# One transformer block on one core: the first layer norm in pairs of blocks, the modulation's scale in four column groups, and a set of weight loads issued from ACT

## The chip, the cores and the metric

The kernel runs on one core of one Trainium2 chip. The metric is device time in microseconds: the median of three runs. A core has engines with instruction queues of their own, which run side by side and wait for each other by semaphores: TensorE (PE, with its weight loads shown as PEld), VectorE (DVE), ScalarE (ACT), GpSimd (POOL) and SyncE (SP). SP does no arithmetic here, it issues DMA transfers; ACT and POOL can issue them too.

## The reference

The reference is one block of depth one over 512 tokens of width 1024: a layer norm modulated by a condition vector, an attention and gating mixer, a second modulated layer norm and a mixture of experts. The change touches the condition's modulation and the first layer norm.

```python
mod = jax.nn.silu(c) @ w_ada[l] + b_ada[l]
sh1, sc1, gt1, sh2, sc2, gt2 = [m[:, None, :] for m in jnp.split(mod, 6, axis=-1)]
h = _layernorm(x) * (1.0 + sc1) + sh1
mix = _token_mixers(h, ...)
x = _layernorm(DN_ALPHA * x + gt1 * mix, ln1_g[l], ln1_b[l])
h = _layernorm(x) * (1.0 + sc2) + sh2
ffn = _peer(h, ...)
x = _layernorm(DN_ALPHA * x + gt2 * ffn, ln2_g[l], ln2_b[l])
```

So mod is a row of six parts of 1024: sh1 and sc1 are wanted at once, before the first projection h @ w_in; the other four later.

## The kernel before

The 512 tokens are four blocks (b = 0 to 3) of 128 rows, x_102 to x_108 in the lists of order below. The width of 1024 is eight chunks of 128 (k = 0 to 7). A projection needs h with the width on the partitions, so x is normalized (L278), transposed by PE in 32 pieces into PSUM (xtr, L283) and copied by ACT to xnT (L284). The modulation is then applied to xnT, one chunk at a time: h_hi (L304) scales and shifts on ACT and casts to the high part hT_h, h_lo (L308) subtracts on DVE for the low part hT_l. Every projection is three products, w_h with hT_h, w_l with hT_h, w_h with hT_l (mm3c, L226), where w_h and w_l are the two parts of a weight that ACT casts (L88) and DVE subtracts (L89). The first projection is w_k: its first half (k = 0 to 3) runs inside the block that the change rewrites, with four accumulators gk, its second half and w_v after it.

The modulation's first two parts, shift (part 0) and scale (part 1), are made in two halves (hf) of 512 columns each, which serve k = 0 to 3 and k = 4 to 7. Each half and part has eight chunks of weights, in two tiles of 1 MB: ada_w for the first half, ada_b for the second, all of them issued by SP (L293). There are two ways to make a row. On DVE (ada_c, L117), eight steps each multiply a chunk by a column of scT (the condition) and add to ada_acc, which ada_t (L108) then sums over the partitions, by PE products with a column of ones (ada_pt) that also turn the row into columns. On PE, eight products with scT as the stationary operand sum straight into one row (ada_row, L313), which ACT copies out. Before, the scale of the first half goes over PE and the three others over DVE; those of the second half stand between the h_lo steps of the first four chunks, and their column sums before the products of k = 3 (L328). ada_e (L299) makes both parts' columns and adds one to the scale (sc1p, L302).

The four later parts are made by ada (L123) in the attention's time: DVE sums into ada_acc, PE sums its partitions in two products of 512 columns with one row out (L135), ACT copies the two rows (L137).

In this first block the order on PE, DVE and ACT is the order of the code; SP's and POOL's orders, and that of all engines outside of such blocks, are set by a scheduler. A DMA transfer tells of its landing by one of eight semaphores (DMAHW0 to DMAHW7), taken in turn in the scheduler's order; the issue of a transfer waits until the earlier transfer with the same semaphore has landed.

Of the kernel before, what the change touches and what calls it, by code (L numbers as in the profile page):

```python
# [9 lines left out]
F32 = mybir.dt.float32  # L10
# [7 lines left out]
ALU = mybir.AluOpType  # L18
# [36 lines left out]
def tile_block(ctx: ExitStack, tc: tile.TileContext, io: dict, out: bass.AP, dbg=None):  # L55
# [52 lines left out]
    def ada_t(acc, part, k0, n):  # L108

        pt = fbank("ada_pt")  # L110
        for c in range(n):
            mm(pt[:, c:c + 1], acc[:, c * P:(c + 1) * P], ones[0:acc.shape[0]], start=True, stop=True)
# [10 lines left out]
    def ada(pl, wl, part, tag, nw):  # L123
# [9 lines left out]
        pr = [fbank("ada_pr") for _ in range(2)]  # L133
        for hf in range(2):
            mm(pr[hf][0:1], ones, acc[:, hf * 512:(hf + 1) * 512], start=True, stop=True)  # L135
        for hf in range(2):
            cp(acc[0:1, hf * 512:(hf + 1) * 512], pr[hf][0:1])  # L137
# [127 lines left out]
    with ExitStack() as es:  # L265
# [8 lines left out]
        with tc.manual_schedule(engines={ET.PE, ET.DVE, ET.Activation}):  # L274
            ln = [(rs, neg(mu, rs)) for mu, rs in ln_stats(xs, D)]
            w_k = [load_w(wp, io["w_k"][0], 408)]
            for b, (rs, nm) in enumerate(ln):
                act(xs[b], xs[b], AF.Identity, scale=rs, bias=nm)  # L278
            for b in range(NB):
                for q in range(2):  # L280
# [3 lines left out]
                    cp(xnT[:, q * 4:q * 4 + 4, b * P:(b + 1) * P], pt.rearrange("p (c t) -> p c t", c=4))  # L284
            bt = [big("ada_b0", F32), big("ada_b1", F32)]
            sc1p = const.tile([P, KC], F32, name="sc1p")
            wa = [[[ap0.tile([P, 4, 512], F32, name="ada_w", bufs=4) for _ in range(2)] for _ in range(2)],
                  [[bt[part][:, c4 * 4:c4 * 4 + 4] for c4 in range(2)] for part in range(2)]]
            acc = [[ap0.tile([P, 512], F32, name="ada_acc", bufs=3) for _ in range(1 + hf)] for hf in range(2)]
            for hf in range(2):  # L290
                for part in range(2):
                    for c4 in range(2):
                        dma(wa[hf][part][c4], io["w_ada01"][hf, part, c4])  # L293

            def ada_cs(hf, part, c0, c1):
                for c in range(c0, c1):
                    ada_c(acc[hf][part], wa[hf][part][c // 4][:, c % 4], c)
# [13 lines left out]
            pr = fbank("ada_row")  # L311
            for c in range(KC):
                mm(pr[0:1], scT[:, c:c + 1], wa[0][1][c // 4][:, c % 4], start=c == 0, stop=c == KC - 1)  # L313
            row = ap0.tile([1, 512], F32, name="ada_row", bufs=1)
            cp(row, pr[0:1])
            acc[0].append(row)
            ada_cs(0, 0, 0, KC)
            ada_cs(1, 0, 0, 4)
            ada_e(0)
            gk = [bank("g") for b in range(NB)]  # L320
# [972 lines left out]
```

## Time and profile before

| | |
|---|---|
| median of 3 runs | 1711.72 us (1710.55 to 1711.78) |
| profiled execution | 1708.1 us |
| its span, first to last instruction | 1706.4 us |
| PE busy | 1660.3 us, 97% |
| DVE busy | 1365.5 us, 80% |
| ACT busy | 663.3 us, 39% |
| PE's idle time before its first transpose | 14.77 us |

An engine's busy time counts its own work and not the issuing of transfers or waiting. The 3% in which PE is not busy are for the most part the start: the first slices of the page show PE at 6 tenths, and every later one at 9 until the last. All times in the rows are from the span's start, for one profiled execution; the runs' median is 3.6 us above it.

### The profile page before, as it was taken

The page shows a single profiled execution, that of the slowest core. Times are in us where ns is not written, and L with a number is a line of the kernel's source. Part 1 is how long each engine was busy: PE and PEld are TensorE (multiplying, and loading weights), DVE is VectorE, ACT ScalarE, POOL GpSimd, SP SyncE. Part 2 cuts the span into 40 slices and gives each one's busy share as a digit, 9 for nine tenths or more (in the row PEclk, how much of TensorE's full clock was granted, in tenths as well). Part 3 has the DMA queues.
Part 4 walks back from the last instruction along what each step waited for, and adds up shares of the span by engine and source line. Part 5 has one row for each costly group of instructions (what it writes and reads, how often), then busy time and mean ns, then how long its engine had stood idle before and what let it go on. Part 6 is the DMA issues. An engine that isn't in the chain of part 4 may idle for free.

```text
span 1706.4 us, 24481 instructions
## 1 busy us (share of the span) xinstructions
PE 1660.3 (97%) x9145; PEld 1434.6 (84%) x9145; DVE 1365.5 (80%) x2682; ACT 663.3 (39%) x1029; POOL 356.7 (21%) x276
## 2 busy tenths in 40 slices
PE   6999999999999999999999999999999999999997
PEld 4977766677888899999998999999999998887785
DVE  6534777758879999998875888888798889788898
ACT  4523532343342244455453333333333334333332
POOL 0000000000000000000011554555454544324310
PEclk9999999999999999999999999999999999999999
DMA  7411344433342145587788999999999999999993
GB/s 307 172 56 50 124 179 155 154 118 136 142 162 79 35 149 168 176 293 263 260 297 321 337 346 359 362 350 355 355 349 345 348 324 347 369 380 384 375 340 121
DMA packets 164478, 424.31 MB, mean 249 GB/s; under 512 B 17283, under 2 KB 84099, under 8 KB 156551
## 3 DMA queue, kind: packets, MB, share of 16 engines
q1 hardware_dynamic: 119159, 277.29, 46.2%
q0 software_dynamic: 36992, 134.25, 21.1%
q10 hardware_dynamic: 8208, 11.21, 1.8%
q8 instruction: 71, 1.16, 0.3%
q14 instruction: 48, 0.39, 0.1%
HBM read 381.59 MB, written 41.11 MB: 248 GB/s over the span
## 4 chain that ended last, share of the span: by engine, by line
PE 88%; DVE 5%; DMA 4%; ACT 1%; issue 1%; SPq 1%; DVEq 0%; ACTq 0%
PE y L1106 24%; PE a_ps L755 10%; PE a_ps L754 10%; PE a_ps L757 10%; PE gf L228 3%; PE gf L229 3%; PE gf L230 3%; PE g_ps L1012 3%; PE s L515 2%; PE qh L782 2%; PE qh L783 2%; PE qh L785 2%; PE oacc L558 2%; DMA gA<-gA_d 1%; DMA v_f<-in_peer_vT_dram 1%; PE g L230 1%
## 5 line engine op out<-in xcount | busy, mean ns | idle before, releaser
L1106 PE MATMUL y<-v_hl,w_eh 128*128 128x512 f32 x1536 | 375.8, 391 | 2.9 <-ACT w_eh L1095 2.6
L754 PE MATMUL a_ps<-h2T_h,u_hl 128*128 128x384 f32 x1024 | 344.2, 336 | 3.1 <-ACT u_hl L88 3.1
L755 PE MATMUL a_ps<-h2T_l,u_hl 128*128 128x384 f32 x1024 | 344.8, 337 | 0.4 <-DVE h2T_l L89 0.3
L1106 PEld LDWEIGHTS y<-v_hl,w_eh 128*128 128x128 f32 x1536 | 287.0, 188 | 63.0 <-ACT w_eh L1095 5.0
L1038 POOL DMA_INDIRECT grow<-in_peer_u_dram,eidx x128 | 172.2, 1345 | 462.1 <-ACT u_hl L88 276.2
L1090 ACT CAST v_hl<-v_f 128x1024 fp32r<-128x1024 f32 x128 | 134.7, 1052 | 266.8 <-PE y L1106 156.6
L1038 POOL DMA_INDIRECT grow<-in_peer_v_dram,eidx x128 | 172.9, 1351 | 224.3 <-DVE yacc L1055 192.5
L757 PE MATMUL a_ps<-h2T_h,u_hl 128*128 128x384 f32 x1024 | 200.3, 335 | 0.0
L1106 PE MATMUL y<-v_hl,w_el 128*128 128x512 f32 x768 | 198.2, 389 | 0.0
L754 PEld LDWEIGHTS a_ps<-h2T_h,u_hl 128*128 128x128 f32 x1024 | 192.3, 188 | 5.7 <-ACT u_hl L88 3.4
L755 PEld LDWEIGHTS a_ps<-h2T_l,u_hl 128*128 128x128 f32 x1024 | 192.3, 188 | 3.3 <-DVE h2T_l L89 1.0
L89 DVE TENSOR_TENSOR u_hl<-u_f,u_hl 128x1024 fp32r<-128x1024 f32 x128 | 156.4, 1222 | 32.8 <-ACT u_hl L88 32.7
L1047 DVE SCALAR_TENSOR_TENSOR grow<-grow,h2t 128x1024 f32<-128x1024 f32 x128 | 153.2, 1223 | 34.0 <-DMA grow<-in_peer_u_dram,eidx 33.5
L757 PEld LDWEIGHTS a_ps<-h2T_h,u_hl 128*128 128x128 f32 x1024 | 179.0, 188 | 0.0
L1055 DVE SCALAR_TENSOR_TENSOR yacc<-grow,dact,yacc 128x1024 f32<-128x1024 f32 x128 | 164.0, 1281 | 18.5 <-DMA grow<-in_peer_v_dram,eidx 17.0
L1096 DVE TENSOR_TENSOR v_hl<-v_f,v_hl 128x1024 fp32r<-128x1024 f32 x128 | 156.2, 1220 | 20.7 <-ACT v_hl L1090 19.0
L1106 PEld LDWEIGHTS y<-v_hl,w_el 128*128 128x128 f32 x768 | 144.1, 188 | 30.2 <-DVE w_el L1097 0.3
L88 ACT CAST u_hl<-u_f 128x1024 fp32r<-128x1024 f32 x128 | 133.8, 1046 | 0.6 <-DMA u_f<-in_peer_uT_dram 0.6
L758 ACT ACTIVATE gA<-a_ps 128x384 f32<-128x384 f32 x119 | 58.4, 491 | 173.3 <-PE a_ps L757 167.7
L1095 ACT CAST w_eh<-gA 128x384 fp32r<-128x384 f32 x119 | 61.1, 514 | 150.5 <-DVE gA L1092 122.6
L1092 DVE TENSOR_TENSOR gA<-gA,g_rd 128x384 f32<-128x384 f32 x119 | 66.0, 554 | 35.0 <-DMA gA<-gA_d 34.1
L228 PE MATMUL gf<-w_h,hT_h 128*128 128x512 f32 x192 | 77.1, 403 | 0.0
(311 smaller groups left out, 2424.1 us busy)
## 6 DMA issues: line engine op xcount, KB each, us to landing
u_f<-in_peer_uT_dram SPq DMA_DIRECT2D x128, 512.0 KB
v_f<-in_peer_vT_dram SPq DMA_DIRECT2D x128, 512.0 KB
gdram<-g_st SPq DMA_DIRECT2D x12, 2048.0 KB
g_rd<-gdram SPq DMA_DIRECT2D x96, 256.0 KB
ada_w<-in_w_ada_dram SPq DMA_DIRECT2D x20, 1024.0 KB
gA_d<-gA ACTq DMA_DIRECT2D x57, 192.0 KB
gA<-gA_d SPq DMA_DIRECT2D x57, 192.0 KB
w_f<-in_w_merge_dram SPq DMA_DIRECT2D x8, 1024.0 KB
```

The lines of the kernel that those rows point to most:

```text
L88: i = cp(hi, src)
L89: V.tensor_tensor(lo, src, hi.bitcast(F32), op=ALU.subtract)
L228: mm(acc, lhs[0][:, k, tb], w[0][:, c, 0:n], start=k == 0, stop=False)
L754: mm(a, wh[:, k], h2T[0][:, k, T0:T0 + TD], start=k == 0, stop=False)
L755: mm(a, wh[:, k], h2T[1][:, k, T0:T0 + TD], start=False, stop=False)
L757: st["u"] = mm(a, wl[:, k], h2T[0][:, k, T0:T0 + TD], start=False, stop=k == KC - 1)
L1038: nc.gpsimd.indirect_dma_start(out=t[:, :], out_offset=None, in_=io["peer_u" if n < P else "peer_v"], in_offset=bass.IndirectOffsetOnAxis( ...
L1047: V.scalar_tensor_tensor(t, t, 1.0, h2t, op0=ALU.mult, op1=ALU.mult, accum_out=G["da"][:, k:k + 1])
L1055: V.scalar_tensor_tensor(yacc, G[P + k], G["da"][:, k:k + 1], yacc, op0=ALU.mult, op1=ALU.add)
L1090: cp(vh, v)
L1096: V.tensor_tensor(vl, v, vh.bitcast(F32), op=ALU.subtract)
L1106: mm(yps[i][hf], w[:, i * P:(i + 1) * P], v[:, hf * 512:(hf + 1) * 512], start=e == 0 and n == 0, stop=e == P - 1 and n == 2)
```

## The change

The first layer norm's statistics are no longer made for all four blocks before the first is normalized. Two blocks at a time are normalized, and their transposes and copies follow; the third and fourth blocks' square roots and normalizations come after copies of the first two on ACT. Each block has its own square root and scale steps (128x1) instead of one set for four (128x4).

The scale (part 1) goes over PE in both halves (ada_row(hf)), the shift (part 0) over DVE in both. The eight products of a row are written to four PSUM rows, 0, 32, 64 and 96, two products each, so that each of four groups of 32 array columns makes one; a memset clears the bank ahead, ACT copies the whole bank, and the sum over partitions in ada_t adds the four rows. In ada the same is done with pieces of 256 columns.

The second half's four weight tiles (ada_b) are issued by ACT, after the normalization of the second block, and no longer by SP. The w_k weights' low part is made in four steps beside h_lo; the second half's DVE steps come after these, its row product before k = 3, its column sums after k = 3.

```diff
-            mm(pt[:, c:c + 1], acc[:, c * P:(c + 1) * P], ones[0:acc.shape[0]], start=True, stop=True)
+            mm(pt[:, c:c + 1], acc[:, c * P:(c + 1) * P], ones, start=True, stop=True)
...
-        pr = [fbank("ada_pr") for _ in range(2)]
-        for hf in range(2):
-            mm(pr[hf][0:1], ones, acc[:, hf * 512:(hf + 1) * 512], start=True, stop=True)
-        for hf in range(2):
-            cp(acc[0:1, hf * 512:(hf + 1) * 512], pr[hf][0:1])
+        pr = fbank("ada_pr")
+        for j in range(4):
+            mm(pr[j * 32:j * 32 + 1, 0:256], ones, acc[:, j * 256:(j + 1) * 256], start=True, stop=True)
+        for j in range(4):
+            cp(acc[0:1, j * 256:(j + 1) * 256], pr[j * 32:j * 32 + 1, 0:256])
...
-            ln = [(rs, neg(mu, rs)) for mu, rs in ln_stats(xs, D)]
-            w_k = [load_w(wp, io["w_k"][0], 408)]
-            for b, (rs, nm) in enumerate(ln):
-                act(xs[b], xs[b], AF.Identity, scale=rs, bias=nm)
-            for b in range(NB):
+            pr = [bank("ada_row") for _ in range(2)]
+            for t in pr:
+                V.memset(t, 0.0)
+            def x_tr(b):
                 for q in range(2):
                     pt = bank("xtr")
...
+            for b0 in range(0, NB, 2):
+                bs = range(b0, b0 + 2)
+                mv = [ln_mv([xs[b]], D) for b in bs]
+                rs = [rsqrt_eps(m[:, :, 1], 1) for m in mv]
+                nm = [neg(m[:, 0, 0:1], r) for m, r in zip(mv, rs)]
+                if b0:
+                    x_tr(b0 - 1)
+                for i, b in enumerate(bs):
+                    act(xs[b], xs[b], AF.Identity, scale=rs[i], bias=nm[i])
+                if b0 == 0:
+                    for part in range(2):
+                        for c4 in range(2):
+                            nc.scalar.dma_start(bt[part][:, c4 * 4:c4 * 4 + 4], io["w_ada01"][1, part, c4])
+                x_tr(b0)
+            x_tr(NB - 1)
+            w_k0 = load_f(wp, io["w_k"][0], 408)
...
-            for hf in range(2):
-                for part in range(2):
-                    for c4 in range(2):
-                        dma(wa[hf][part][c4], io["w_ada01"][hf, part, c4])
+            for part in range(2):
+                for c4 in range(2):
+                    dma(wa[0][part][c4], io["w_ada01"][0, part, c4])
...
+            def ada_row(hf):
+                for c in range(KC):
+                    j = c % 4 * 32
+                    mm(pr[hf][j:j + 1], scT[:, c:c + 1], wa[hf][1][c // 4][:, c % 4], start=c < 4, stop=c >= 4)
+                cp(acc[hf][1], pr[hf])
...
-            pr = fbank("ada_row")
-            for c in range(KC):
-                mm(pr[0:1], scT[:, c:c + 1], wa[0][1][c // 4][:, c % 4], start=c == 0, stop=c == KC - 1)
-            row = ap0.tile([1, 512], F32, name="ada_row", bufs=1)
-            cp(row, pr[0:1])
-            acc[0].append(row)
-            ada_cs(0, 0, 0, KC)
-            ada_cs(1, 0, 0, 4)
+            ada_cs(0)
...
+            cp(wh[:, :, 0:408], w_k0[:, :, 0:408])
+            ada_row(0)
             ada_e(0)
...
             for k in range(4):
-                for i in range(k * 3, k * 3 + 3):
-                    ada_cs(1, int(i > 3), (i + 4) % 8, (i + 4) % 8 + 1)
+                V.tensor_tensor(wl[:, k, 0:408], w_k0[:, k, 0:408], wh[:, k, 0:408].bitcast(F32), op=ALU.subtract)
                 h_lo(k)
+            ada_cs(1)
+            for k in range(4):
                 if k == 3:
-                    ada_e(1)
+                    ada_row(1)
                 for b in range(NB):
                     mm3c(gk[b][:, 0:408], hT, b, w_k[0], k, k, 408, KC)
+            ada_e(1)
```

Three places show how the instructions now stand. The first is the start of ACT's queue, after the condition's own steps; ln_rs is the square root, x_102 to x_108 the four blocks, ada_b the second half's weights, and the names after "waits" are the semaphores. Before:

```order
L153 ACTIVATE ln_rs_128<-ln_mv_114,eps_76 128x4 [waits DVE_49]
L88 CAST w_h<-w_f 128x4x408 [waits DMAHW6_49]
L278 ACTIVATE x_102<-x_102,ln_n,ln_rs_128 128x1024 [waits DMAHW2_49,DVE_49]
L278 ACTIVATE x_104<-x_104,ln_n,ln_rs_128 128x1024 [waits DMAHW3_49,DVE_49]
L278 ACTIVATE x_106<-x_106,ln_n,ln_rs_128 128x1024 [waits DMAHW4_49,DVE_49]
L278 ACTIVATE x_108<-x_108,ln_n,ln_rs_128 128x1024 [waits DMAHW5_49,DVE_49]
L284 COPY xnT<-xtr 128x4x128 [waits PE_49] x8
L315 COPY ada_row<-ada_row 1x512 [waits PE_49]
```

And of the changed kernel, the same stretch of ACT's queue:

```order
L296 ACTIVATE x_102<-x_102,ln_n,ln_rs_130 128x1024 [waits DMAHW2_49,DVE_49]
L296 ACTIVATE x_104<-x_104,ln_n,ln_rs_138 128x1024 [waits DMAHW3_49,DVE_49]
L301 DMA ada_b_117<-in_w_ada_dram 128x2048 [waits DMAHW7_49]
L301 DMA ada_b_117<-in_w_ada_dram 128x2048 [waits DMAHW0_49]
L301 DMA ada_b_118<-in_w_ada_dram 128x2048 [waits DMAHW1_49]
L301 DMA ada_b_118<-in_w_ada_dram 128x2048 [waits DMAHW2_49]
L285 COPY xnT<-xtr 128x4x128 [waits PE_49] x2
L154 ACTIVATE ln_rs_178<-ln_mv_168,eps_76 128x1 [waits DVE_49]
L154 ACTIVATE ln_rs_186<-ln_mv_173,eps_76 128x1 [waits DVE_49]
L285 COPY xnT<-xtr 128x4x128 [waits PE_49] x2
L296 ACTIVATE x_106<-x_106,ln_n,ln_rs_178 128x1024 [waits DMAHW4_49,DVE_49]
L296 ACTIVATE x_108<-x_108,ln_n,ln_rs_186 128x1024 [waits DMAHW5_49,DVE_49]
```

The four issues of ada_b, each with a wait for a semaphore, now stand between the second block's normalization and the first copy of a transposed block. The second place is SP's queue of the changed kernel from its first transfer on, which tells whose semaphores those are: the ninth transfer takes DMAHW0 a second time.

```order
L100 DMA cT<-in_cT_dram 128x8
L102 DMA b_ada<-in_b_adaT_dram 128x16
L272 DMA x_102<-in_x_dram 128x1024
L272 DMA x_104<-in_x_dram 128x1024
L272 DMA x_106<-in_x_dram 128x1024
L272 DMA x_108<-in_x_dram 128x1024
L215 DMA w_f<-in_w_k_dram 128x4x408
L311 DMA ada_w<-in_w_ada_dram 128x2048
L311 DMA ada_w<-in_w_ada_dram 128x2048 [waits DMAHW0_49]
L311 DMA ada_w<-in_w_ada_dram 128x2048 [waits DMAHW1_49]
L311 DMA ada_w<-in_w_ada_dram 128x2048 [waits DMAHW2_49]
L215 DMA w_f<-in_w_k_dram 128x4x408 [waits DMAHW3_49]
```

Counted from cT at DMAHW0, ada_w's four take DMAHW7, 0, 1 and 2, the last three of them for the second time. Where ada_b's four issues followed ada_w's in SP's queue before, with waits for DMAHW3 to DMAHW6, the second w_k load now stands. The third place is PE's queue around the last chunk (k = 3) of w_k's first half. Before:

```order
L112 MATMUL ada_pt<-ones,ada_acc 128x1 x8
L228 MATMUL g<-w_h,hT_h 128x408
L229 MATMUL g<-w_l,hT_h 128x408
L230 MATMUL g<-w_h,hT_l 128x408
L228 MATMUL g<-w_h,hT_h 128x408
```

And of the changed kernel, from the end of those products on:

```order
L231 MATMUL g<-w_h,hT_l 128x408
L112 MATMUL ada_pt<-ones,ada_acc 128x1 x8
L229 MATMUL g<-w_h,hT_h 128x384 x2
L229 MATMUL g<-w_h,hT_h 128x408 x4
L230 MATMUL g<-w_l,hT_h 128x408 x4
L230 MATMUL g<-w_l,hT_h 128x384
```

The column sums stood before the twelve products of k = 3 and stand behind them; the row product of the second half has their old place. After them come two products of w_v (384 columns) and then those of k = 4.

## Rows read from the trace of the kernel before

**Rows 1.** The page's first part: busy time and share of the span by engine.

```profile
PE 1660.3 (97%) x9145; PEld 1434.6 (84%) x9145; DVE 1365.5 (80%) x2682; ACT 663.3 (39%) x1029; POOL 356.7 (21%) x276
```

**Rows 2.** PE's waits: who waited for whom, us in total, times, longest.

```profile
PE xtr L283 <- ACT x L278: 14.8, 1, 14.8
```

**Rows 3.** PE's timeline: start, length (us), line, work, count, [idle before].

```profile
14.77 6.20 PE L283 MATMUL xtr<-ident,x 128*128 128x128 f32 x32 [14.77 <-ACT x L278]
20.90 7.03 PE L313 MATMUL ada_row<-ada_w,scT 128*1 128x512 f32 x16
...
31.91 0.71 PE L228 MATMUL g<-w_h,hT_h 128*128 128x408 f32 x1 [2.02 <-ACT hT_h L306]
...
41.31 1.84 PE L112 MATMUL ada_pt<-ones,ada_acc 128*128 128x1 f32 x16
...
45.31 0.90 PE L228 MATMUL g<-w_h,hT_h 128*128 128x408 f32 x4
```

**Rows 4.** SP's timeline, its issues.

```profile
4.34 2.33 SPq L293 DMA_DIRECT2D ada_w<-in_w_ada_dram  x4
6.78 5.34 SPq L293 DMA_DIRECT2D ada_b<-in_w_ada_dram  x4
14.30 0.57 SPq L214 DMA_DIRECT2D w_f<-in_w_k_dram  x1
16.77 0.34 SPq L459 DMA_DIRECT2D cmask<-in_cmask_dram  x1
19.28 2.76 SPq L461 DMA_DIRECT2D rvalid<-in_rvalid_dram  x1
```

**Rows 5.** The waits of SP's queue.

```profile
SPq L461 <- DMA ada_w<-in_w_ada_dram: 2.2, 1, 2.2
```

**Rows 6.** ACT's timeline.

```profile
11.74 0.30 ACT L153 ACTIVATE ln_rs<-ln_mv,eps 128x4 f32<-128x4 f32 x1 [7.78 <-DVE ln_mv L173]
11.95 1.53 ACT L88 CAST w_h<-w_f 128x1632 fp32r<-128x1632 f32 x1
13.39 4.63 ACT L278 ACTIVATE x<-x,ln_n,ln_rs 128x1024 f32<-128x1024 f32 x4
17.93 3.95 ACT L284 COPY xnT<-xtr 128x512 f32<-128x512 f32 x8
27.96 0.57 ACT L315 COPY ada_row<-ada_row 1x512 f32<-1x512 f32 x1 [6.09 <-PE ada_row L313]
30.39 0.81 ACT L305 ACTIVATE xnT<-xnT,modT,sc1p 128x512 f32<-128x512 f32 x1 [1.85 <-DVE sc1p L302]
```

**Rows 7.** DVE's timeline.

```profile
12.07 0.18 DVE L155 RECIPROCAL ln_t<-ln_rs 128x4 f32<-128x4 f32 x1 [0.16 <-ACT ln_rs L153]
...
15.80 5.48 DVE L121 SCALAR_TENSOR_TENSOR ada_acc<-ada_w,scT,ada_acc 128x512 f32<-128x512 f32 x7
...
43.47 1.86 DVE L89 TENSOR_TENSOR w_l<-w_f,w_h 128x1632 fp32r<-128x1632 f32 x1
...
47.18 1.76 DVE L89 TENSOR_TENSOR w_l<-w_f,w_h 128x1536 fp32r<-128x1536 f32 x1 [1.25 <-ACT w_h L88]
```

**Rows 8.** DMA queues from 1301 to 1302.5 us: packets, MB, engines' share.

```profile
q0 software_dynamic: 82, 0.33, 55.0%
q1 hardware_dynamic: 72, 0.27, 45.2%
```

**Rows 9.** The chain of waits at the start: start, us, what.

```profile
1.74 3.72 DMA x<-in_x_dram
```

**Rows 10.** PE's timeline, a later part's partition sums.

```profile
222.76 1.02 PE L135 MATMUL ada_pr<-ada_acc,ones 128*1 128x512 f32 x2
```

**Rows 11.** PE's timeline, products in two groups of 64 columns.

```profile
382.38 1.09 PE L634 MATMUL mix<-sw,z 128*64 128x128 f32 x16
```

**Rows 12.** Windows: length, busy by engine, granted clock, DMA share, GB/s.

```profile
30.00:35.00 5.00, 2.87 (x7) 2.28 (x8) 4.86 (x10) 4.52 (x7) 0.00 (x0) 0.52 1.03 366
```

More of the change, by code (lines that the diff above doesn't have):

```diff
@@ L288, in tile_block, with ada_cs @@
                   [[bt[part][:, c4 * 4:c4 * 4 + 4] for c4 in range(2)] for part in range(2)]]
-            acc = [[ap0.tile([P, 512], F32, name="ada_acc", bufs=3) for _ in range(1 + hf)] for hf in range(2)]
-            for hf in range(2):
-                for part in range(2):
-                    for c4 in range(2):
-                        dma(wa[hf][part][c4], io["w_ada01"][hf, part, c4])
-            def ada_cs(hf, part, c0, c1):
-                for c in range(c0, c1):
-                    ada_c(acc[hf][part], wa[hf][part][c // 4][:, c % 4], c)
+            acc = [[ap0.tile([P, 512], F32, name="ada_acc", bufs=4) for _ in range(2)] for hf in range(2)]
+            for part in range(2):
+                for c4 in range(2):
+                    dma(wa[0][part][c4], io["w_ada01"][0, part, c4])
+            def ada_cs(hf):
+                for c in range(KC):
+                    ada_c(acc[hf][0], wa[hf][0][c // 4][:, c % 4], c)
+            def ada_row(hf):
+                for c in range(KC):
+                    j = c % 4 * 32
+                    mm(pr[hf][j:j + 1], scT[:, c:c + 1], wa[hf][1][c // 4][:, c % 4], start=c < 4, stop=c >= 4)
+                cp(acc[hf][1], pr[hf])
             def ada_e(hf):
@@ L309, in h_lo @@
                 V.tensor_tensor(hT[1][:, k], xnT[:, k], hT[0][:, k].bitcast(F32), op=ALU.subtract)
-            pr = fbank("ada_row")
-            for c in range(KC):
-                mm(pr[0:1], scT[:, c:c + 1], wa[0][1][c // 4][:, c % 4], start=c == 0, stop=c == KC - 1)
-            row = ap0.tile([1, 512], F32, name="ada_row", bufs=1)
-            cp(row, pr[0:1])
-            acc[0].append(row)
-            ada_cs(0, 0, 0, KC)
-            ada_cs(1, 0, 0, 4)
+            ada_cs(0)
+            wh = wp.tile([P, 4, 512], F32R, name="w_h", tag="w_h", bufs=2)
+            wl = wp.tile([P, 4, 512], F32R, name="w_l", tag="w_l", bufs=2)
+            w_k = [(wh, wl)]
+            cp(wh[:, :, 0:408], w_k0[:, :, 0:408])
+            ada_row(0)
             ada_e(0)
```

## The prediction

> **What bounds the kernel now.** I read the page first: PE is busy 97% of the span [rows 1], so a microsecond is worth a microsecond only where PE stands still or is given other work. The list of PE's waits has one long entry, 14.8 us before its first transpose [rows 2]; everything else on that list is short. The change touches the stretch after that wait, so I read PE's timeline next [rows 3]: transposes from 14.77, the modulation's row product (ada_row) from 20.90 to 27.93, the column sums (ada_pt), a gap of 2.02 us, and from 31.91 the first projection (g), after which PE does not stop until the work of the first 70 us is done. So the date to watch is 31.91: what moves it moves the end, one for one, and so does PE work added or taken away behind it. ACT's row at 30.39 is the step that sets it, the first scaled block h_hi; the first g starts 1.52 us later [rows 3, 6]. I call the start of h_hi H; before it is 30.4.
>
> **What the change adds: a hold on ACT.** Each transfer takes the next of eight semaphores, and an issue waits until the earlier transfer on its semaphore has landed. SP's timeline shows what that does [rows 4]: its issues at 14.30, 16.77 and 19.28 each waited for one of the four ada_w transfers, 2.5 us (1 MB at 0.42 MB per us) apart, and the list of SP's waits names ada_w as what ended them, the last after 2.2 us [rows 5]. Nothing on SP but later transfers stood behind these. In the changed order the four ada_b issues stand on ACT, and they wait for semaphores 7, 0, 1 and 2, which by the order on SP are ada_w's first to fourth transfer. Behind them on ACT stand all eight copies of the transposed x, the second pair's square roots and its two normalizations. So ACT cannot copy the first transposed block before ada_w's fourth transfer has landed. Before, that was at 19.28 + 2.5 = 21.8. ACT could be there at 13: the four blocks' statistics run from x's landing at 5.46 [rows 9] to 11.74 [rows 6], 1.57 a block, so two are done at 8.6, and ten small DVE steps (2.0) and two normalizations (2.4) follow.
>
> No row of before shows ACT's own queue held by such a wait. [...]
>
> **How long the hold is.** The first ada_b is issued at 14.3, when ada_w's first has landed. The first block of x, 0.5 MB, takes 3.72 us from issue to landing [rows 9], of which its bytes are 1.25; of the other 2.5 I put 1.4 ahead of the first byte and 1.1 behind the last. So ada_b's bytes start at 15.7, when ada_w's second (landed at 16.77) is just read. If the two queues share the engines evenly, ada_w's third and fourth each take 5.0 us instead of 2.5: read at 20.7 and 25.7, landed at 21.8 and 26.8. With 0.34 for the last issue (as SP's at 16.77) [rows 4] ACT is free at T = 27.1. If SP's transfers went first, T = 21.8 + 0.3 = 22.1. The nearest row is a stretch in which two queues both had work: 0.33 MB on one and 0.27 MB on the other, 55% and 45% of the engines' time [rows 8]. I take even sharing, T = 27.1, and keep 22.1 as the low end: the last issue waits for the last ada_w, so lower it cannot be. At the high end an issue that stalls as SP's at 19.28 did (2.76 us) [rows 4] gives 29.
>
> [...]
>
> **From T to H.** Two copies at 0.49 (3.95 for 8) [rows 6], 1.0; a square root, 0.3 [rows 6]; then DVE's chain for a pair, eight small steps to the first scale at 0.2 each (0.18 and the step to the next) [rows 7], 1.65: the third block is normalized from T + 2.95. At 1.2 us for it (4.63 for 4) plus 0.15, PE transposes from T + 4.3; sixteen at 0.21, the pace that they begin with [rows 3], end at T + 7.75. Then ada_row: 16 passes which took 0.43 each at full clock (7.03 in all), in four column groups. If these run side by side it is four rounds, 1.9 at full clock and 3.7 at half; the clock rises somewhere in it, so I take 2.75, ending at T + 10.6. ACT has copied and cast w_h (1.53) [rows 6] by T + 10.0, and DVE's eight ada_acc steps (5.5 for seven, so some 6) [rows 7], which start after the pair's chain at T + 3.1, end at T + 9; both are hidden by PE, and cost up to 1 us each if ada_row takes 1.9. From ada_row's end to H the steps are as before, a copy of 0.57 and 1.86 more (27.96 + 0.57 = 28.53 to 30.39) [rows 6]: H = T + 13.1, between T + 12.4 and T + 14.7. That is 40.2, against 30.4: **+9.8 us**.
>
> The first pair's early normalization, the memsets of two PSUM banks (DVE has nothing until x comes) and the ten more small DVE steps lie under the hold and gain or cost nothing of their own. Without the hold they would be what pays.
>
> **The first projection.** PE gets a second ada_row, for the second half's scale, ahead of k = 3: **+1.9**, and DVE loses its eight steps for that, which PE did not wait for. The column sums of the second half (1.84) [rows 3] move behind k = 3. Before, the twelve matmuls of k = 3 (43.1 to 45.31, 2.2 us) [rows 3] covered the way from them over the scale to hT of k = 4. Now PE has two w_v matmuls (0.4) to run there. The scale takes 0.45 and hT 1.5, so PE stands **1.6**. Then w_l of w_k's second half (1.86) and w_l of w_v (1.76) [rows 7] come after the scale on DVE: ready 0.3 + 1.86 + 1.76 = 4.0 after the column sums end, while PE has eight more matmuls and gets there at 3.5: **+0.5**. DVE's second ada_acc chain ends at H + 12, before the column sums at H + 15. Together +4.0; between 1.9 (the scheduler's other fillers cover the waits) and 5. PE's clock is taken as before: it was 0.52 of full speed in 30 to 35 us [rows 12], and 36 matmuls took 9.4 us where 12 at full clock take 2.2, so 2.8 us are lost there; if the clock is up when g starts, that much comes back, and if it rises later up to 1.7 more goes.
>
> **The later rows.** Each of four parts had four passes of 512 columns, 1.02 us for two [rows 10], so 4 x 0.43 + 0.2 = 1.9. Eight passes of 256 columns in four groups are two rounds of 0.21, with 0.2 for the change-over 0.6. PE is without gaps there, so 4 x 1.3 = **-5.2**. What speaks for groups side by side is the row of the two halves of 64 columns: sixteen passes of 128 columns in 1.09 us [rows 11], of which the last one's own length is 0.27; 0.055 apart where 0.107 would be the pace of 0.43 for 512. That shows two, not four. Bounds: 0 (none overlaps) and -5.2. ACT makes four copies of 256 instead of two of 512: at most 2 x 0.57 more a part [rows 6], hidden by an ACT that is 39% busy [rows 1]; uncovered, +4.6.
>
> **Sum.** 9.8 + 4.0 - 5.2 = +8.6. On the profiled execution, 1708.1 us with a span of 1706.4, that is 1716.7; the median of the runs is 1711.7, 3.6 above the profiled one, so 1720.
>
> **Rivals.**
> 1. The hold, but SP's transfers go first: T = 22.1, H = 35.2, +4.8 + 4.0 - 5.2 = +3.6, 1715. For it: SP's are issued first. Against: [rows 8].
> 2. The faster end: ACT's queue sets the waiting issues aside, and the transfers behind ada_w do not slow it. Then the copies go on at 13, the second pair's transposes end near 21, ada_row's second half starts when ada_w has landed (21.8) and ends at 23, and with w_h's cast and the steps to H it is 26.5: -3.9 + 4.0 - 5.2 = -5, 1706.6. It decides if ACT's first copy starts before 18. Against it: every issue on SP waited in its place. If the issues go ahead but share evenly from 13 on, ada_w is in at 29, H about 33, and the sum is +1.5, no change.
> 3. The four groups run one after the other: ada_row is 7.0 twice and the later rows gain nothing, +4.3 + 5.1 + 5.2 on the forecast, 1735. If only two overlap: about +5, 1725. Against it: [rows 11]; for it: no row has four groups.
>
> **Chances.** Forecast 0.55, rival 1 0.17, rival 2 0.10 with its even-sharing form 0.05, rival 3 0.13. A measurement of this kernel tells about 0.2%, 3.4 us, from no change. The forecast and rival 3 are slower; rival 1 lies on the border and is split; the even-sharing form is no change. Slower 0.76, same 0.15, faster 0.09. For the range: the forecast's own terms run from T + 12.4 with 1.9 in the projection (1717.5) to T = 29 with T + 14.7 (1724); below it reaches to rival 1 at its low ends, 22.1 + 12.4 and 1.9 (1712.5), and above to two groups with a late clock (1728).
>
> **What would show it.** The hold: ACT idle from about 13 to 27, its issues of ada_b each at the landing of an ada_w, PE idle between the second block's transposes and T + 4. Sharing: ada_w's third and fourth 5 us apart. The groups: ada_row's sixteen passes within 2 to 4 us. The projection: PE waiting on hT after the second column sums. The later rows: passes of 256 columns in bunches of four starts. The forecast is wrong if ACT copies before 18 us, if g starts before 36, or if the stretch after 70 us does not shift by what g's start does.

## The result, and the profile after

The changed kernel takes 1721.98 us (median of 10 runs, 1716.99 to 1729.2) where the kernel before takes 1710.73 beside it: a ratio of 1.0067, with a 95% interval of 1.0052 to 1.0082. It is slower by 11.3 us; the forecast was 1720. Its profiled execution took 1720.53 us, with a span of 1718.8.

The page's first part, to be held against [rows 1]: PE's busy time has not grown, the span has. The time went into waiting.

```profile
PE 1658.0 (96%) x9177; PEld 1435.5 (84%) x9177; DVE 1361.1 (79%) x2690; ACT 666.8 (39%) x1041; POOL 350.0 (20%) x276
```

PE's timeline of the first 62 us, against [rows 3] (start, length, line, work, count, [idle before and what ended it]). In place of one wait of 14.77 us there are two, 11.37 and 14.62; the first g stands at 39.04 instead of 31.91. The sixteen passes of the row product take 1.92 and 1.90 instead of 7.03.

```profile
11.37 3.65 PE L284 MATMUL xtr<-ident,x 128*128 128x128 f32 x16 [11.37 <-ACT x L296]
29.63 3.67 PE L284 MATMUL xtr<-ident,x 128*128 128x128 f32 x16 [14.62 <-ACT x L296]
33.23 1.92 PE L322 MATMUL ada_row<-ada_w,scT 128*1 128x512 f32 x16
35.08 1.95 PE L112 MATMUL ada_pt<-ones,ada_acc 128*128 128x1 f32 x16
39.04 0.46 PE L229 MATMUL g<-w_h,hT_h 128*128 128x408 f32 x1 [2.01 <-ACT hT_h L332]
...
47.81 1.90 PE L322 MATMUL ada_row<-ada_b,scT 128*1 128x512 f32 x16
...
51.96 1.84 PE L112 MATMUL ada_pt<-ones,ada_acc 128*128 128x1 f32 x16
...
55.76 1.01 PE L229 MATMUL g<-w_h,hT_h 128*128 128x408 f32 x4 [1.45 <-ACT hT_h L332]
```

ACT's timeline and its queue, against [rows 6]. The four issues start at 14.74, 17.24, 20.36 and 25.33, each at the landing of an ada_w, and the first copy, which PE's transposes had made possible by 12.6 (e1 below has it there), comes at 25.70: 13.35 us of idle time, ended by ada_w. That is the hold. ada_w's first two landings are 2.5 apart, the third comes 3.1 later, the fourth 5.0.

```profile
9.98 2.37 ACT L296 ACTIVATE x<-x,ln_n,ln_rs 128x1024 f32<-128x1024 f32 x2 [0.93 <-DVE ln_n L186]
14.74 0.38 ACTq L301 DMA_DIRECT2D ada_b<-in_w_ada_dram  x1
17.24 0.34 ACTq L301 DMA_DIRECT2D ada_b<-in_w_ada_dram  x1
20.36 0.33 ACTq L301 DMA_DIRECT2D ada_b<-in_w_ada_dram  x1
25.33 0.34 ACTq L301 DMA_DIRECT2D ada_b<-in_w_ada_dram  x1
25.70 1.07 ACT L285 COPY xnT<-xtr 128x512 f32<-128x512 f32 x2 [13.35 <-DMA ada_w<-in_w_ada_dram]
...
37.52 0.81 ACT L331 ACTIVATE xnT<-xnT,modT,sc1p 128x512 f32<-128x512 f32 x1 [1.66 <-DVE sc1p L328]
```

The sharing, from the DMA queues between 18 and 23 us (packets, MB, share of the engines; q1 carries what SP issues, q10 what ACT issues). ada_b's first bytes move at 18.2, 3.5 behind its first issue; in this stretch each queue has half of the engines, and ada_w's fourth landing comes 5.0 behind its third where the first two were 2.5 apart.

```profile
q1 hardware_dynamic: 147, 1.05, 50.9%
q10 hardware_dynamic: 131, 1.04, 49.6%
```

A window of the same profile (length, busy time of PE, PEld, DVE, ACT and POOL, granted clock, DMA share, GB/s). From 20 to 25 us no engine computes at all, and the DMA engines are full (1.02).

```profile
20.00:25.00 5.00, 0.00 (x0) 0.00 (x0) 0.00 (x0) 0.00 (x0) 0.00 (x0) 1.00 1.02 423
```

PE's timeline at two of the four later parts, against [rows 10]. One part's eight passes stand together (0.54 from their start to the work behind), in the other the scheduler has put two by themselves, and each bunch costs what the eight cost.

```profile
235.13 0.61 PE L136 MATMUL ada_pr<-ada_acc,ones 128*1 128x256 f32 x8
235.68 0.54 PE L584 MATMUL oacc<-p_T,v 128*64 128x128 f32 x5
...
268.71 0.59 PE L136 MATMUL ada_pr<-ada_acc,ones 128*1 128x256 f32 x2
269.24 0.55 PE L575 MATMUL pT<-ident,p_r 128*128 128x128 f32 x3
269.71 0.60 PE L136 MATMUL ada_pr<-ada_acc,ones 128*1 128x256 f32 x6
270.25 0.55 PE L575 MATMUL pT<-ident,p_r 128*128 128x128 f32 x3
```

### The profile page after: what moved, and what is told of

Read it like the earlier page. It is cut to its first block, busy times and chain, and to the rows that moved or that the text cites. A ratio compares the mean times of both kernels' runs of the same rounds, so it can differ in the third digit from the quotient of the medians.

```text
span 1718.8 us, 24567 instructions
## 1 busy us (share of the span) xinstructions
PE 1658.0 (96%) x9177; PEld 1435.5 (84%) x9177; DVE 1361.1 (79%) x2690; ACT 666.8 (39%) x1041; POOL 350.0 (20%) x276
## 4 chain that ended last, share of the span: by engine, by line
PE 44%; issue 17%; DVE 14%; DMA 14%; POOL 8%; ACT 2%; SPq 1%; POOLq 0%; ACTq 0%; DVEq 0%
POOL grow L1064 7%; DMA grow<-in_peer_v_dram,eidx 4%; DMA gA<-gA_d 4%; PE a_ps L780 3%; PE a_ps L781 3%; PE a_ps L783 3%; DMA v_f<-in_peer_vT_dram 3%; PE gf L229 3%; PE gf L230 3%; PE gf L231 3%; PE g_ps L1038 2%; DVE yacc L1081 2%; PE y L1132 2%; DVE v_hl L1122 2%; PE s L541 2%
## 5 line engine op out<-in xcount | busy, mean ns | idle before, releaser
L1064 POOL DMA_INDIRECT grow<-in_peer_v_dram,eidx x128 | 166.2, 1298 | 230.7 <-DVE yacc L1081 205.4
```

Of the source, the lines that this page charges most:

```text
L1064: nc.gpsimd.indirect_dma_start(out=t[:, :], out_offset=None, in_=io["peer_u" if n < P else "peer_v"], in_offset=bass.IndirectOffsetOnAxis( ...
```

## The experiments

The theory: ACT is held by its own four issues, the sharing of the engines makes that longer, and the new order in the projection costs less than 4. The rivals: the sharing alone is the loss; the new work is; or the groups of columns don't overlap. Ratios are to the kernel before, run on the same chip beside each.

**Who issues, and where.** Three kernels move the four issues of ada_b and leave the rest of the changed kernel as it is.

`e1_sp_issue`:
```diff
-                if b0 == 0:
-                    for part in range(2):
-                        for c4 in range(2):
-                            nc.scalar.dma_start(bt[part][:, c4 * 4:c4 * 4 + 4], io["w_ada01"][1, part, c4])
...
                     dma(wa[0][part][c4], io["w_ada01"][0, part, c4])
+            for part in range(2):
+                for c4 in range(2):
+                    dma(wa[1][part][c4], io["w_ada01"][1, part, c4])
```

> The changed kernel with one thing undone: SP issues the second half's weights (ada_b), behind the four ada_w. Theory (the loss is ACT's queue held by the four issues): ACT copies the first transposed block at about 13 us instead of 25.7, the first h_hi comes at 26.5 to 28 instead of 37.5, the first g near 28.5 instead of 39.0, so about 10.5 us less than the changed kernel's 1722: 1711 (1708 to 1714), level with the kernel before. Rival (the loss lies in the new work itself, the paired layer norm, the second row product and the groups of columns): the start does not move the end, 1719 to 1722.

Measured: 1711.21 us, ratio 1.0007 (0.9988 to 1.0026). PE's timeline: the second pair's transposes follow the first's after 1.81 us, PE waits 0.74 for ada_w's last, and the first g is at 27.49, 11.6 before the changed kernel's. The first h_hi is at 25.98. The rival falls: the new work is all there, and the 10 us are not.

```profile
16.98 3.68 PE L284 MATMUL xtr<-ident,x 128*128 128x128 f32 x16 [1.81 <-ACT x L296]
20.59 1.23 PE L320 MATMUL ada_row<-ada_w,scT 128*1 128x512 f32 x8
22.56 1.04 PE L320 MATMUL ada_row<-ada_w,scT 128*1 128x512 f32 x8 [0.74 <-DMA ada_w<-in_w_ada_dram]
...
27.49 0.45 PE L229 MATMUL g<-w_h,hT_h 128*128 128x408 f32 x1 [2.02 <-ACT hT_h L330]
```

`e2_act_late`:
```diff
-                if b0 == 0:
...
             x_tr(NB - 1)
+            for part in range(2):
+                for c4 in range(2):
+                    nc.scalar.dma_start(bt[part][:, c4 * 4:c4 * 4 + 4], io["w_ada01"][1, part, c4])
```

> The changed kernel, ACT still issues ada_b, but behind its last copy of the transposed x. Theory (only the place in ACT's queue matters): nothing but w_h's cast stands behind the issues, the copies run from about 13, the issues come at about 20 and the last of them goes out when ada_w's last has landed, near 22 to 24; first h_hi at 27 to 29.5, 1711 to 1714. Rival (it is ACT as issuer, or the two queues sharing the 16 engines, that costs): the first h_hi stays above 33, 1717 or more.

Measured: 1715.28 us, ratio 1.0037 (1.0017 to 1.0057). ACT's timeline has the four issues behind its copies, done within 1.84 us, and the first h_hi at 26.12:

```profile
20.60 1.84 ACTq L301 DMA_DIRECT2D ada_b<-in_w_ada_dram  x4
...
26.12 0.81 ACT L329 ACTIVATE xnT<-xnT,modT,sc1p 128x512 f32<-128x512 f32 x1 [1.61 <-DVE sc1p L326]
```

So ACT may issue without holding the start; it is the place in its queue that holds it. The start is e1's, and so is the profiled span (1707.9 against 1707.6), but the median is 4 above e1's and outside the expectation. Set against each other, the twelve runs of each kernel differ by 4.9 in the mean, give or take 3.5, so the difference is probably real. Its cause stays open: the two single profiles don't have it at their ends.

`e3_pool_issue`:
```diff
+                        nc.gpsimd.tensor_copy(bt[part][:, 0, 0:1], xs[1][:, 0:1])
+                        nc.gpsimd.tensor_copy(bt[part][:, 4, 0:1], xs[1][:, 0:1])
...
-                            nc.scalar.dma_start(bt[part][:, c4 * 4:c4 * 4 + 4], io["w_ada01"][1, part, c4])
+                            nc.gpsimd.dma_start(bt[part][:, c4 * 4:c4 * 4 + 4], io["w_ada01"][1, part, c4])
```

> The changed kernel with ada_b issued by POOL at about 13 us, when the second block of x is normalized (four copies of one column on POOL make it wait for that). So the two queues share the engines as in the changed kernel, from a little earlier, but nothing on ACT waits. Theory (hold): ACT copies from about 13; ada_w's last lands late, at 25 to 29, because of the sharing, and ada_row waits for it; first h_hi at 29 to 32, 1713 to 1717. Rival (sharing is the whole loss): first h_hi at 36 to 38 as in the changed kernel, 1720 to 1722.

Measured: 1720.0 us, ratio 1.0053 (1.0032 to 1.0074), the first h_hi at 35.62. That is nearly the rival's number, and the theory's was missed. ACT was free, though, as expected, and ada_w was in at 27.3. DVE's timeline shows what else there is: a cast of a mask that nothing needs for long stands ahead of the scale's steps, and DVE is held 13.28 us for the mask's transfer of 64 KB. SP had issued that at 12.37, ahead of POOL's four (from 13.1), but DVE's wait for it ends only at 34.95, 22.6 later. The changed kernel's trace has the mask's transfer at 22.5 us from issue to landing, and there the queues of SP and ACT move 323 packets each from 25 to 32 us, 0.53 MB of SP's against 2.38 MB of ACT's.

```profile
34.95 0.23 DVE L494 CAST dmask<-dmask_f 128x128 bf16<-128x128 f32 x1 [13.28 <-DMA dmask_f<-in_dmask_dram]
35.09 0.22 DVE L115 TENSOR_TENSOR modT<-ada_pt,b_ada 128x4 f32<-128x4 f32 x2
```

So this run doesn't tell sharing and hold apart: it has the sharing and a hold on another engine. The next one takes that away, and issues at about the times of the changed kernel (15.41, 18.07, 20.43 and 25.36). It was run twice.

`e9_pool_stagger`, `e13_pool_stagger2`:
```diff
+            for i in range(4):
+                part, c4 = i // 2, i % 2
+                nc.gpsimd.tensor_copy(bt[part][:, c4 * 4, 0:1], wa[0][part][c4][:, 0, 0:1])
+                nc.gpsimd.dma_start(bt[part][:, c4 * 4:c4 * 4 + 4], io["w_ada01"][1, part, c4])
...
-    V.tensor_copy(dmask, dmask_f)
+    nc.gpsimd.tensor_copy(dmask, dmask_f)
```

> The changed kernel with each ada_b issued by POOL when the ada_w that the changed kernel's issue waits for has landed (a copy of one column on POOL makes it wait), so at about 14.7, 17.2, 20.4 and 25.3, and dmask's cast on POOL as well, where DVE doesn't wait for it. The sharing is then as in the changed kernel and ACT waits for nothing. Theory (the hold is most of the loss): ACT copies from 13; PE waits for ada_w's last at 25.3, first h_hi at 28.5 to 31, so sharing is 3 to 5 of the 11.5 between SP's issue and ACT's. Rival (sharing is all of it, and in the run with POOL issuing at 13 it was not dmask's cast on DVE that came last): first h_hi at 35 to 38.

> The kernel in which POOL issues each ada_b as the changed kernel's ACT does, once more, for its time. With the first h_hi at 30.8 between 26.0 (SP issues) and 37.5 (ACT issues), theory: between the two, 1714 to 1717, ratio 1.002 to 1.005. Rival (what stands on ACT behind the issues matters, but only the end of the sharing counts for the end of the program): as the changed kernel, 1.0065.

Measured: 1712.87 us in the one run of the first; 1713.58 us and a ratio of 1.0009 (0.9992 to 1.0026) in the second, below its expectation. The first one's rows, ACT's ahead of PE's: PE waits 3.31 for ada_w's last, which is in at 24.8 (25.3 in the changed kernel), and the first h_hi is at 30.75 (31.08 in the second).

```profile
30.75 0.81 ACT L330 ACTIVATE xnT<-xnT,modT,sc1p 128x512 f32<-128x512 f32 x1 [3.35 <-DVE sc1p L327]
```

```profile
24.86 1.88 PE L321 MATMUL ada_row<-ada_w,scT 128*1 128x512 f32 x8 [3.31 <-DMA ada_w<-in_w_ada_dram]
26.68 3.57 PE L112 MATMUL ada_pt<-ones,ada_acc 128*128 128x1 f32 x16
32.27 0.71 PE L229 MATMUL g<-w_h,hT_h 128*128 128x408 f32 x1 [2.01 <-ACT hT_h L331]
```

By the date of the first h_hi the loss at the start divides so: 25.98 with SP's issue, 30.75 with nearly the same sharing and no hold (+4.8), 37.52 with the hold (+6.8). Of the 4.8, 2.3 are ada_w's later landing: PE's last passes of ada_row start at 24.86, in e1 at 22.56. The other 2.5 go with PE's pace behind its wait: the last eight passes take 1.88 where e1's take 1.04, and ada_pt 3.57 instead of 1.95. The changed kernel's ada_pt took 1.95 at a granted clock of 1.00, and e9's first g takes 0.71, as in the kernel before [rows 3], where 0.50 was granted from 31.9 to 35.0 us. The whole times agree for the hold, 1.0009 against 1.0057 and 1.0067; sharing's 4.8 is not seen between e1 and e13, whose intervals are 3 us wide to each side.

**The hold alone, in the kernel before.** `e6_before_hold`:
```diff
                 act(xs[b], xs[b], AF.Identity, scale=rs, bias=nm)
+            bt = [big("ada_b0", F32), big("ada_b1", F32)]
+            for part in range(2):
+                for c4 in range(2):
+                    nc.scalar.dma_start(bt[part][:, c4 * 4:c4 * 4 + 4], io["w_ada01"][1, part, c4])
             for b in range(NB):
...
-            for hf in range(2):
+            for hf in range(1):
                 for part in range(2):
                     for c4 in range(2):
                         dma(wa[hf][part][c4], io["w_ada01"][hf, part, c4])
```

> The kernel before with one thing of the change alone: ACT issues ada_b, behind its four normalizations and ahead of its eight copies. Theory (hold): the first copy waits for ada_w's last, which sharing brings to about 25; PE's last transposes and its sixteen row products (7.0) stand behind the copies, first h_hi near 36 instead of 30.4: 1715 to 1719. Rival (an issue that waits does not stop the work behind it on ACT): first h_hi at 30 to 31.5, 1710 to 1712.

Measured: 1724.67 us, ratio 1.0087 (1.0062 to 1.0113). The theory's mechanism is there, the first copy at 25.49 where the kernel before has it at 17.93 [rows 6]; its price is larger than expected. The sharing comes with the hold in this run, so the price is that of both. PE's timeline: after 7.09 us of standing, ada_row takes 8.79 instead of 7.03, and the first g is at 40.80, 8.9 later than before.

```profile
26.13 1.97 PE L287 MATMUL xtr<-ident,x 128*128 128x128 f32 x8 [7.09 <-ACT xnT L288]
28.03 8.79 PE L316 MATMUL ada_row<-ada_w,scT 128*1 128x512 f32 x16
...
40.80 0.46 PE L228 MATMUL g<-w_h,hT_h 128*128 128x408 f32 x1 [2.02 <-ACT hT_h L309]
```

The window from 62 to 470 us shows a granted clock of 0.97 on the mean, against 0.99 and 0.98 in the two profiles of before: by an estimate of 4 us for each hundredth (1% of the 408), some 4 to 8 us more. With the 8.9 (9.9 against the second profile) that is 14 to 17, where the ratio gives 14.9. That the hold brings the lower clock isn't shown: the changed kernel, with the hold, has 0.99 there.

**The groups of columns.** `e8_one_group` makes the row products one after another:
```diff
-                    j = c % 4 * 32
-                    mm(pr[hf][j:j + 1], scT[:, c:c + 1], wa[hf][1][c // 4][:, c % 4], start=c < 4, stop=c >= 4)
+                    mm(pr[hf][0:1], scT[:, c:c + 1], wa[hf][1][c // 4][:, c % 4], start=c == 0, stop=c == KC - 1)
```

> The changed kernel with both row products (ada_row) in one group of array columns instead of four: eight passes after one another for a half's scale. What it tells: whether the four groups run side by side, which is what the forecast assumed. Theory (they do): the first sixteen records take 7.0 at full clock instead of 1.92, and the second sixteen 6.9 instead of 1.90, both on the path: first g near 44, 9 to 11 more than the changed kernel by 62 us, 1730 to 1733 where the changed kernel is at 1720 to 1722. Rival (the rows of the changed kernel are short only because their ends are modelled): no change at all, 1720 to 1722.

Measured: 1740.59 us, ratio 1.0164 (1.0135 to 1.0193). The rival falls, and without the groups the kernel is 19.5 slower than the changed one beside it (1721.07, below), more than the 10 us of the passes themselves. PE's timeline has the passes at 7.24 and 7.03:

```profile
34.14 7.24 PE L321 MATMUL ada_row<-ada_w,scT 128*1 128x512 f32 x16
...
53.50 7.03 PE L321 MATMUL ada_row<-ada_b,scT 128*1 128x512 f32 x16
```

The rest goes with PE's clock. This window of the same kernel and that of the changed kernel's second profile show 0.96 against 0.99 granted between 62 and 470 us, by the same estimate 12 us of that stretch; with the passes' own 10 that is a little over the 19.5. What lowers the clock there isn't shown.

```profile
62.00:470.00 408.00, 396.43 (x2194) 300.40 (x2193) 254.00 (x499) 159.01 (x300) 7.18 (x9) 0.96 0.37 129
```

```profile
62.00:470.00 408.00, 400.47 (x2240) 302.87 (x2239) 265.04 (x532) 158.51 (x306) 7.30 (x9) 0.99 0.37 129
```

The four groups gave 7.03 / 1.90 = 3.7 in the second set of passes. The 1.90 were at a granted clock of 1.00, and so were the kernel before's sixteen passes in one group, which took 7.03 too [rows 3].

**The later rows alone.** `e5_before_new_rows` is the kernel before with the new ada:
```diff
-        pr = [fbank("ada_pr") for _ in range(2)]
-        for hf in range(2):
-            mm(pr[hf][0:1], ones, acc[:, hf * 512:(hf + 1) * 512], start=True, stop=True)
...
+        pr = fbank("ada_pr")
+        for j in range(4):
+            mm(pr[j * 32:j * 32 + 1, 0:256], ones, acc[:, j * 256:(j + 1) * 256], start=True, stop=True)
```

> The kernel before with the later rows of the change alone: four column groups of 256 instead of two products of 512 columns. The traces so far give 0.95 from one product of a pair to the work behind the pair, eight pairs, 7.6 in all, against 3.2 for the four bunches of the changed kernel. Theory (PE's time is the end's time there): 4.4 less than before, 1704 to 1707 where before is at 1709 to 1711. Rival (the four small copies on ACT, or a gap opened behind them, take it back): within 1 of before.

Measured: 1710.74 us, ratio 1.0010 (0.9995 to 1.0026): no gain in the whole time. For the place where it went, a landmark helps: the first transposes after the attention's output, one row in every profile. Here it is for the kernel before, for its second profile (the next run), for the changed kernel, its second profile, and e5:

```profile
470.82 1.09 PE L198 MATMUL tr<-ident,xn 128*128 128x128 f32 x8 [0.93 <-ACT xn L724]
```

```profile
472.48 1.09 PE L198 MATMUL tr<-ident,xn 128*128 128x128 f32 x8 [0.93 <-ACT xn L724]
```

```profile
478.15 1.09 PE L199 MATMUL tr<-ident,xn 128*128 128x128 f32 x8 [0.94 <-ACT xn L750]
```

```profile
480.20 1.09 PE L199 MATMUL tr<-ident,xn 128*128 128x128 f32 x8 [0.94 <-ACT xn L750]
```

```profile
468.01 1.09 PE L199 MATMUL tr<-ident,xn 128*128 128x128 f32 x8 [0.94 <-ACT xn L725]
```

At 470 us e5 is 2.8 ahead of the one profile of before and 4.5 ahead of the other, so most or all of the 4.4 is there. Later it loses some: PE stands at 706.27 for 0.79, on DVE's u_hl.

```profile
706.27 1.68 PE L758 MATMUL a_ps<-h2T_h,u_hl 128*128 128x384 f32 x8 [0.79 <-DVE u_hl L89]
```

The same stop of 0.79, with a different order of PE's work around it, is in the changed kernel (below), in e1, e2, e3, e6, e9 and e13 (in e7 it is 1.24), and in neither profile of before, nor in e8 and the last run. The scheduler lays that stretch out anew when the work ahead of it changes. Besides, e5's granted clock is 0.50 from 482.6 to 485.8 us, where both profiles of before have 1.00 on the mean from 470 to 690: 1.6 more. That is 2.4 of the 4.4. The theory is missed: the interval reaches to 0.9 below the kernel before and not to 4.4, and where the rest goes isn't shown.

**Both kernels once more.** `e10_before_again` and `e11_after_again` are the two kernels unchanged.

> The kernel before once more, unchanged, for a second profile of it. The changed kernel's shift against the first profile is 7.3 at 480 us and 12.4 at the end. Theory (the rest is not the change's: PE's clock falls or does not fall behind the same gaps near 485 and 905 us): this profile shows the clock at 0.5 for 3.4 us near 484 or 907, which the first one does not, and a span 1.7 or 3.4 above 1706.4. Rival (the rest belongs to the change): no such stretch, span 1706 to 1707.

> The changed kernel once more, unchanged, on the chip of these runs. Theory: ACT's first copy at 25.7, first h_hi at 37.5 and first g at 39.0 within 0.5 as before, and a ratio to the kernel before of 1.005 to 1.008. The shift behind 480 us, 5 in the first profile, is free to differ: between 2 (the stretch of 700 to 740 us alone) and 8, by where PE's clock falls and by the waits of the last stage.

Measured: before, one run, 1718.11 us with a span of 1716.4, the longest run of this kernel on record (the others reach 1717.66); after, 1721.07 us, ratio 1.0057 (1.0037 to 1.0076). So the kernel before itself has a profile 10.0 longer than the first, with the first g at 30.92 instead of 31.91. The expected fall of the clock near 907 is there (a granted clock of 0.50 from 912), one near 484 is not; and PE's waits of the last stage, from 1370 us on, are 6.5 against 2.6 in the first profile:

```profile
912.10:915.40 3.30, 3.30 (x13) 3.30 (x12) 2.04 (x3) 0.51 (x1) 0.00 (x0) 0.50 0.68 205
```

```profile
PE y L1106 <- ACT w_eh L1095: 6.5, 5, 2.2
```

Shifts behind 480 us in single profiles are therefore no evidence on the change, but for what both profiles of the changed kernel have and neither of before. The changed kernel's second profile has the hold again, with ada_row slower (2.63 for the sixteen passes instead of 1.92; the granted clock of the first 62 us is 0.81 on the mean, 0.97 in the first profile):

```profile
26.49 1.07 ACT L285 COPY xnT<-xtr 128x512 f32<-128x512 f32 x2 [13.99 <-DMA ada_w<-in_w_ada_dram]
...
39.03 0.81 ACT L331 ACTIVATE xnT<-xnT,modT,sc1p 128x512 f32<-128x512 f32 x1 [1.71 <-DVE sc1p L328]
```

**Towards a faster one.** `e7_sp_mid_e` is e1 with the second column sums ahead of the third block of k = 3, and the mask's cast on POOL:
```diff
                 for b in range(NB):
+                    if k == 3 and b == 2:
+                        ada_e(1)
                     mm3c(gk[b][:, 0:408], hT, b, w_k[0], k, k, 408, KC)
-            ada_e(1)
```

> The changed kernel with ada_b issued by SP, the second half's column sums in the middle of k = 3 (ahead of its third block) instead of behind it, and dmask's cast on POOL, where nothing waits for dmask's transfer. Theory: first h_hi at 26 as with SP's issue alone, and the wait of 1.45 on hT goes, as DVE's second chain is done at 38.5 and twelve more matmuls cover the way to hT: 1 to 2 less than with SP's issue alone, about 1709. Rival (the column sums wait for DVE's chain in the middle of k = 3): no gain, a wait of 1 to 1.5 at the column sums instead.

Measured: 1710.32 us, ratio 1.0011 (0.9996 to 1.0027), as e1. Neither theory nor rival: the column sums wait for nothing, and the wait on hT is replaced by one on a weight's cast, which the scheduler has put behind the first scaled block on ACT.

```profile
40.07 1.84 PE L112 MATMUL ada_pt<-ones,ada_acc 128*128 128x1 f32 x16
44.69 1.35 PE L229 MATMUL g<-w_h,hT_h 128*128 128x384 f32 x3 [1.56 <-ACT w_h L88]
```

`e12_wk_behind` is e1 with w_k's first half behind the four ada_w, and its cast on ACT behind the copy of ada_row:
```diff
-            w_k0 = load_f(wp, io["w_k"][0], 408)
...
                     dma(wa[0][part][c4], io["w_ada01"][0, part, c4])
+            w_k0 = load_f(wp, io["w_k"][0], 408)
...
-            cp(wh[:, :, 0:408], w_k0[:, :, 0:408])
             ada_row(0)
+            cp(wh[:, :, 0:408], w_k0[:, :, 0:408])
```

> The best start that the runs point to: SP issues ada_b, and w_k's first half goes behind the four ada_w instead of ahead of them, its cast on ACT behind the copy of ada_row. Theory: ada_w's last lands 2 earlier, at 20, so PE goes from its last transposes into ada_row without a wait; first h_hi at 24.8 instead of 26.0, 1 less than with SP's issue alone: ratio 0.996 to 1.001 to the kernel before. Rival (w_l of w_k's first half is late instead, as its bytes land at 22): PE waits at its second or third matmul, no gain.

Measured: 1707.14 us, ratio 0.9970 (0.9952 to 0.9987): faster than both kernels. PE goes from the transposes into ada_row without a wait, the first h_hi is at 25.01, and the first g at 26.53, 5.4 before the kernel before. That start is 1.0 ahead of e1's, but by the ratios the kernel is 6.3 faster than e1. The stop near 706 us is gone (PE is busy in all of the 55 us from 690), which is 0.8 of it; the rest isn't explained.

```profile
16.96 3.05 PE L284 MATMUL xtr<-ident,x 128*128 128x128 f32 x16 [1.91 <-ACT x L296]
19.94 2.70 PE L320 MATMUL ada_row<-ada_w,scT 128*1 128x512 f32 x16
...
26.53 0.71 PE L229 MATMUL g<-w_h,hT_h 128*128 128x408 f32 x1 [2.01 <-ACT hT_h L330]
```

## Why the prediction was right, and where its sizes were off

- **The hold** was right in kind and in place: ACT's copies wait for ada_w's fourth transfer, behind issues that each start at a landing. That a waiting issue holds ACT was carried over from SP's rows [rows 4, 5], and the 13.35 us of ACT's idle time show it. T was put at 27.1 and is 25.70 and 26.49 in the two profiles. The third ada_w takes 3.1 instead of the 5.0 worked out, the fourth 5.0 as worked out: the first ada_b's bytes were put 1.4 behind its issue, which was an estimate, and came 3.5 behind it, at 18.2. Rival 1 (SP's transfers first, T = 22.1) and rival 2 (issues set aside, a first copy before 18) are out; e9 shows that with the hold gone the copies do run at 12.65.
- **From T to H**: 13.1 was forecast, 11.8 and 12.5 measured. The term most off is ada_row, 2.75 in the sum, an estimate between full and half clock: it took 1.92 at a granted clock of 1.00 in one profile, 2.63 in the other; the rest is some tenths in the steps on either side. H came to 37.52 and 39.03 instead of 40.2, so the start costs 7.1 and 8.6, not 9.8 (8.1 and 9.6 against the second profile of before, whose h_hi is at 29.40).
- **The first projection**: +4.0 was forecast. From the first g to the first product of the second half it is 55.76 - 39.04 = 16.72, where before had 45.31 - 31.91 = 13.40 [rows 3]: +3.3. The granted clock is 0.90 on the mean over the one stretch and 0.81 over the other, which gives back 0.9, as the prediction said it might; so the work itself added some 4.2. The second ada_row (1.90) and the wait on hT (1.45 where 1.6 was put) are as forecast. The 0.5 for w_l is 0.19 in the profile; e7 shows that the wait on hT can't be had for nothing.
- **The later rows**: -5.2 was forecast. The groups overlap (7.03 against 1.90 for sixteen passes, e8), so the bound was the right one, but two of the four parts' bunches were split in two. From the start of a bunch to the work behind it, the four take 0.54, 1.06, 1.06 and 0.54, 3.2 in all, where the eight pairs of before took 0.95 each: -4.4. e5 shows that in its place, and no gain in the whole time.
- **The sum** to 470 us: 7.1 + 3.3 - 4.4 = 6.0 by the first profile, where the forecast had 8.6. The landmark shows the changed kernel 7.3 behind the first profile of before and 5.7 behind the second; its second profile is 9.4 and 7.7 behind. Of the prediction's signs of being wrong, a copy before 18 and a g before 36 didn't come; the third holds the shift against g's start alone and leaves out the sum's own +4.0 and -5.2.
- **Behind 470 us** the forecast had nothing, and something is there: the stop at 716.47, which the order of the changed kernel brings. The window of 690 to 745 us shows PE 54.02 busy of 55, where both profiles of before have 55.00. The changed kernel's first profile also has a granted clock of 0.50 from 494.2 to 497.5 us, 1.7 more; from 470 to 690 us the mean is 0.99 in both its profiles and 1.00 in both of before. Nor is the start most of what PE stood idle before, as was said ahead of the prediction: 17 of some 46 us lie in the first 62.

```profile
716.47 1.66 PE L783 MATMUL a_ps<-h2T_h,u_hl 128*128 128x384 f32 x8 [0.79 <-DVE u_hl L89]
```

The end, 11.3 (8.9 to 14.0) and in the second set 9.7 (6.3 to 13.0), is a little above that sum. What fills the difference in the runs' median isn't settled; it is of the size by which two profiles of one kernel differ there.

That the total came so near the forecast is in part luck: the start was put up to 2.7 too high, and what came behind 470 us was put at nothing. Its premise that what moves the first g, or PE's work behind it, moves the end one for one isn't borne out by every run. e1 has its first h_hi at 25.98, as rival 2 had put it (26.5), but rival 2's sum of -5 is not there: +1.2 by the ratio, between -2.1 and +4.4. e5 takes 4.4 from PE's work and has +1.7, between -0.9 and +4.4. e12, with a start like e1's, has -5.1. Why the end follows in one and not in the others isn't known.

That the new start is good without the hold was said in the prediction ("would be what pays"). e1 shows it in the first h_hi (25.98 instead of 30.39) and not in the whole time; e12 is faster, but w_k's load has moved there too. Issuing from ACT had a price in this case's rows: 0.34 per issue, and 10.9 from the first to the last.

## What to carry to other kernels

An issue put on an engine that also computes stands in that engine's queue, and here four of them held ACT for 13.35 us: before moving one, look at which earlier transfer its semaphore still carries, and at what stands behind it in that queue. Put it behind the work it would hold (e2) or leave it on a queue that does nothing else (e1, the faster of the two here). When only order changes, read the end of the profile too: the scheduler lays later stretches out anew, and a gain of 4 in its place need not be there at the end (e5).

## What the runs showed of the hardware that was not expected

- A hold isn't ACT's alone: in e3 a mask's cast held DVE for 13.28 us. The mask's 64 KB were issued at 12.37, ahead of POOL's 4 MB (from 13.1) and on another queue, and DVE's wait for them ended at 34.95.
- Two queues with work shared the engines by packets here rather than by bytes: in the changed kernel 147 and 131 packets for 1.05 and 1.04 MB from 18 to 23 us, but 323 and 323 for 0.53 and 2.38 MB from 25 to 32 us, where SP's packets were 1.6 KB on the mean and ACT's 7.4.
- The mean granted clock between 62 and 470 us is 0.96 to 0.99 in these kernels, by estimate 4 us for each hundredth, and a stop at the start doesn't tell which: the changed kernel, with a stop of 14.62, has 0.99 in both profiles, e6 with 7.09 has 0.97, e1 without a hold 0.98, e8 with the changed kernel's hold 0.96. What makes the difference was not tried.
- The same instructions took different times in two profiles of one kernel: ada_row 1.92 in one, 2.63 in the other, with 0.97 and 0.81 as the mean granted clock of the first 62 us.
